# Projections in five pieces of 512 columns, gate and up with sixteen little products in a row, and a planner that knows the turns of VectorE and GpSimd

## The chip, the core and the metric

One core of a Trainium2 chip runs the whole program in one launch. The metric is the device time in microseconds (us) of one execution. TensorE multiplies matrices into PSUM, ScalarE (ACT) and VectorE (DVE) work elementwise on SBUF and PSUM, GpSimd (POOL) works elementwise on SBUF, and SyncE (SP) issues most of the DMAs.

## What is computed

Two encoder layers over 256 tokens of width 1024, in float32. Cut to what matters:

```python
def mixer_sublayer(x, ...):
    proj = rms_norm(x, n1) @ w_in_l                      # 1024 -> 2560 columns
    qa, ka, va, qd, kd, vd, qc, kc, vc = split(proj)     # 4+4+4, 6+6+6, 6+2+2 heads of 64
    out_a = neighbourhood_attention(norm(qa), norm(ka), va, rpb)
    out_d = dilated_window_attention(rope(norm(qd)), rope(norm(kd)), vd)
    out_c = gqa_block_attention(rope(norm(qc)), rope(norm(kc)), vc)
    mix = concat(rms_norm(out_a), rms_norm(out_d), rms_norm(out_c))
    return x + mix @ w_out_l

def channel_sublayer(x, ...):
    g, u = split(rms_norm(x, n2) @ w_gu)                 # 1024 -> 2 x 2816
    g = depthwise_conv_centred(g, cw, cb)                # three taps along the tokens
    return x + (gelu(g) * u) @ w_dn
```

## The kernel before

**Precision.** Every float32 operand is split into a large part `hi` (a cast to fp32r) and a rest `lo`. A product a·b is three matmuls, hi·hi, hi·lo and lo·hi (`mm3`). ScalarE makes `hi` of each weight chunk (`wp_hi`), VectorE the rest (`wp_lo`). The token rows lie in two tiles t of 128.

**Projections.** `PROJ` cuts the 2560 columns of `w_in` into seven pieces: dq, dk, dv and cq of 384 columns, ckv of 256, aqk of 512, av of 256. A piece takes 2 (t) × 8 (k, chunks of 128 rows) × 3 matmuls into two PSUM banks of the pool `psa`, with the split activations `act_hT` as weights in the array and the split `w_in` streaming through it. A load unit is one DMA into a `raw` buffer (four exist): four chunks k of a piece of 384 or 512 columns, eight of a piece of 256.

**Attention.** The `weave` runs the projections, and after them the output projections (`act_mixT` with `w_out`), as filler between the steps of 16 heads: norm and rotation of queries and keys (`normed`, `rotated`, tile `act_z`), transposes (`transposed`), score products with half the array (64 rows), softmax, transposes of the probabilities, and weighing of the values (`const_v`). For the dilated heads `rotated` takes tables that GpSimd makes from the norm gains (`tables_d`).

**Gate and up.** `half_up` makes two PSUM banks j = 0, 1 of the pool `psw`. For each bank there are eight large products (wp_hi with both parts of `act_hT`, 512 columns) and eight little ones (wp_lo with the large part, 256 columns). The order is large 0, little 0, large 1, little 1. There are 22 calls in each layer; the first of a layer has an order of its own. `down` stands between them, with 24 products of 512 columns for two tiles j.

**Order.** Nothing runs as it is written: the class `Plan` records all operations, and `order` lists them by estimated start times from `cost`, with hand-written shifts of rank in `PLACES`. Every engine then works through its own list strictly in order. `LANDS` holds the times at which the planner takes the first loads to be landed. All recorded operations carry the line L472, the call in `emit`, so the profile is read by tile names.

```python
            for j in range(2):
                for k in range(KD):
                    large(j, k)
                for k in range(KD):
                    little(j, k)
```

Of the kernel before, what the change touches and what calls it, by code (L numbers as in the profile page):

```python
# [18 lines left out]
P = 128  # L19
# [32 lines left out]
LANDS = (4100, 3300, 5300, 3450, 5800, 6450, 7250, 8200, 8900, 9800, 10700, 10750, 10800)  # L52
# [4 lines left out]
SUM_ACT, SCALE_ACT = ("dq", "dk", "cq"), ("dk",)  # L57
# [9 lines left out]
PROJ_NAMES = ["dq", "dk", "dv", "cq", "ckv", "aqk", "av"]  # L67
PROJ = [
    (_CD, _WD), (_CD + _WD, _WD), (_CD + 2 * _WD, _WD), (_CC, H_GQ * HD),
    (_CC + H_GQ * HD, 2 * GKV_W), (0, 2 * H_NA * HD), (2 * H_NA * HD, H_NA * HD),  # L70
]

OUTP = [(2, 3), (5, 3), (0, 2)]
# [132 lines left out]
class Op:  # L206
    __slots__ = ("engine", "method", "args", "kw", "ns", "lat", "kind", "size", "tiles", "first", "before", "after", "left", "at", "rank", "burst")
# [17 lines left out]
def handover(a, b):  # L225
# [13 lines left out]
class Plan:  # L239
# [30 lines left out]
    def add(self, engine, method, args, kw):  # L270
# [16 lines left out]
        o.ns, o.lat, o.size, o.kind = cost(engine.name, method, args, kw, ins)  # L287
        func = args[2] if method == "activation" else None
# [34 lines left out]
    def order(self):  # L323
# [9 lines left out]
        wires = {}  # L333
        ready = {e: [] for e in ("PE", *free)}
# [68 lines left out]
        while len(done) < len(ops):  # L403
# [71 lines left out]
def cost(engine, method, args, kw, ins):  # L475
# [11 lines left out]
    if engine == "PE":  # L487
        if method == "transpose":
            return n / 2.25 + 2.5, 0, 0, "turn"
        n = args[2].width()  # L490
        ns = {512: 231.6, 384: 174.5, 256: 118.0}.get(n, n / 2.25 + 2.5)
# [14 lines left out]
    elif method == "tensor_copy":  # L506
        ns = 0.92 * n + 100
    elif kw.get("op") == ALU.pow:
        ns = 560 + 150 * n
    elif method == "tensor_scalar":  # L510
        ns = 350 + 3.8 * n
    else:
        ns = 830 if out.width() == S else 350 + 3.1 * n
    return ns, ns - 95, 0, None


@with_exitstack
def encoder_kernel(
# [70 lines left out]
    with nc.later(1000):  # L589
# [8 lines left out]
        [const.tile([P, NT, 2 * n + 1, HD], F32R, tag=f"v{n}{i}", name=f"v{n}{i}") for i in range(2)]  # L598
        for n in (H_DIL, H_GKV)
    )  # L600
    for z in vown + vkv:
        nc.gpsimd.memset(z[:, :, 0::2].bitcast(F32), 0.0)

    def rows(w, k0, n, c0, width):
        return w[k0 * P : (k0 + n) * P, c0 : c0 + width].rearrange("(k p) c -> p k c", p=P)

    def units_of(l):

        for c0, width in PROJ:
            per = 4 if width * 8 > UNIT else 8  # L610
            for k0 in range(0, KD, per):
                yield rows(w_in[l], k0, per, c0, width)
        for gi, c0 in OUT_ORDER:
            yield rows(w_out[l], *OUTP[gi], c0, 512)
        for kind, s in FFN:
            if kind == "D":
                yield rows(w_down[l], 2 * s, 2, 0, D)
            else:
                yield rows(w_gate_up[l], 0, KD, (D_FF if kind == "U" else 0) + s * 2 * P, 2 * P)
# [8 lines left out]
    def keep(i):  # L628
        v = views[i]
        a, b = v.shape[1], v.shape[2]  # L630
        n = a * b
        raw = wp.tile([P, UNIT], F32, tag="raw", name=f"raw{i}", bufs=RAWS)
        nc.sync.dma_start(raw[:, :n].rearrange("p (a b) -> p a b", b=b), v)
# [10 lines left out]
    def load(i):  # L644
        v = views[i]
        a, b = v.shape[1], v.shape[2]
# [10 lines left out]
        rv = raw[:, : a * b].rearrange("p (a b) -> p a b", b=b)  # L657
        if i == 0:
            for by, what, c in START:
                by = nc.scalar if by == "act" else nc.sync  # L660
                if what == "w":
                    by.dma_start(rv[:, c], v[:, c])
# [7 lines left out]
        else:  # L670
            for c in range(0, a, 2 if i == 1 else a):
                e = c + 2 if i == 1 else a
                nc.sync.dma_start(rv[:, c:e], v[:, c:e])
        raws.append(raw)

    def places_of(i):
# [4 lines left out]
        return (16, 16) if views[i].shape[2] == 2 * P else (0, 0)  # L681

    def split(i):
        v = views[i]
        a, b = v.shape[1], v.shape[2]
# [170 lines left out]
    def tables_d(l, which):  # L856
        cd = act.tile([P, NT, HD], F32, tag=f"cd{which}", name=f"cd{which}{l}", bufs=1)
        sd = small.tile([P, NT, 16], F32, tag=f"sd{which}", name=f"sd{which}{l}", bufs=1)
        b = lambda v: v.unsqueeze(1).to_broadcast([P, NT, v.shape[1]])
        nc.gpsimd.tensor_tensor(cd, gains_of["rot"][:, :, 0:64], b(gains_of[which][:, l, 1]), op=ALU.mult)  # L860
        for i in range(2):
            o, n = (8 * i, 8 * (1 - i)), 8
            nc.gpsimd.tensor_tensor(
                sd[:, :, o[0] : o[0] + n],
                gains_of["rot"][:, :, 64 + o[0] : 64 + o[0] + n],
                b(gains_of[which][:, l, 1, o[1] : o[1] + n]),
                op=ALU.mult,
            )
        return cd, sd
# [21 lines left out]
    def tables_of(l):  # L891
        for which in "qk":
            tables["d" + which, l] = tables_d(l, which)
# [4 lines left out]
    for l in range(DEPTH):  # L898
# [11 lines left out]
        def projections():  # L910
            for (c0, width), name in zip(PROJ, PROJ_NAMES):
# [649 lines left out]
```

## Time and profile before

| | us |
|---|---|
| median of 3 runs | 604.35 (604.31 to 604.79) |
| the profiled execution | 604.39 |
| its span, first to last instruction | 602.6 |
| PE busy in the span | 596.9 (99%), 3496 matmuls |
| DVE busy | 484.9 (80%) |
| ACT busy | 428.5 (71%) |
| POOL busy | 81.0 (13%) |

The profiled execution is the span and 1.8 us around it. Busy times of PE are unions of overlapping matmuls, each of which is drawn with its way through the array; how fast the array takes matmuls is read from the distance of their starts.

### The profile page before, as it was taken

How to read it: one execution, taken by the hardware profiler on the slowest of the kernel's cores; microseconds unless marked ns; L12 is line 12 of the kernel's file. 1: busy time of each engine (PE TensorE's matmuls, PEld its weight loads, DVE VectorE, ACT ScalarE, POOL GpSimd, SP SyncE). 2: the span in 40 equal slices, each digit the busy share in tenths (PEclk: the TensorE clock that was granted, in tenths of full speed). 3: DMA queues.
4: the chain of work that ended last, by engine and by line, in shares of the span. 5: the costliest groups of instructions: out<-in, count | busy, mean ns of one | idle time of the engine just before them, and what ended most of it. 6: DMA issues, size and time to landing. Idle time of an engine off the chain costs nothing.

```text
span 602.6 us, 9916 instructions
## 1 busy us (share of the span) xinstructions
PE 596.9 (99%) x3496; PEld 524.7 (87%) x3496; DVE 484.9 (80%) x995; ACT 428.5 (71%) x1065; POOL 81.0 (13%) x130
## 2 busy tenths in 40 slices
PE   8999999999999999999999999999999999999997
PEld 7999898888888888888899989888888888888886
DVE  4899988997788988888777898777977777777775
ACT  6889999686566767666688899676766556666661
POOL 2733030102400000000023213421000000000000
PEclk9999999999999999999999999999999999999999
DMA  8893313557588898999444726844465556555501
GB/s 281 294 329 114 106 36 108 196 188 238 174 243 292 274 358 310 327 308 298 155 143 159 258 71 245 281 177 140 140 210 202 171 188 210 173 179 208 194 16 70
DMA packets 85218, 121.44 MB, mean 202 GB/s; under 512 B 9881, under 2 KB 69881, under 8 KB 85169
## 3 DMA queue, kind: packets, MB, share of 16 engines
q1 hardware_dynamic: 82896, 112.17, 55.8%
q0 software_dynamic: 1728, 8.39, 4.1%
q8 instruction: 27, 0.44, 0.3%
q10 hardware_dynamic: 544, 0.26, 0.1%
q14 instruction: 23, 0.18, 0.1%
HBM read 110.93 MB, written 9.88 MB: 200 GB/s over the span
## 4 chain that ended last, share of the span: by engine, by line
PE 97%; ACT 1%; DVE 1%; POOL 0%; issue 0%; DVEq 0%; POOLq 0%
PE psw_w L472 53%; PE psa_a L472 44%; ACT act_s2k L472 0%; POOL small_rstd L472 0%; ACT act_z L472 0%; DVE act_z L472 0%; ACT act_hT L472 0%; DVE wp_lo L472 0%; DVE act_sw L472 0%; POOL small_ms L472 0%; DVE const_x L472 0%; DVE act_qo L472 0%; ACT wp_hi L472 0%; POOL const_warm L472 0%; DVEq L472 0%
## 5 line engine op out<-in xcount | busy, mean ns | idle before, releaser
L472 DVE TENSOR_TENSOR wp_lo<-wp_raw,wp_hi 128x512 fp32r<-128x512 f32 (+2 forms) x332 | 231.8, 733 | 57.1 <-ACT wp_hi L472 41.1
L472 ACT CAST wp_hi<-wp_raw 128x512 fp32r<-128x512 f32 (+2 forms) x332 | 203.0, 663 | 21.7 <-PE psw_w L472 10.1
L472 PE MATMUL psw_w<-act_hT,wp_hi 128*128 128x512 f32 x704 | 180.3, 393 | 0.0
L472 PEld LDWEIGHTS psw_w<-act_hT,wp_hi 128*128 128x128 f32 x704 | 127.3, 188 | 24.5 <-DVE act_hT L472 0.6
L472 PE MATMUL psa_a<-wp_hi,act_hT 128*128 128x384 f32 (+2 forms) x448 | 112.6, 331 | 0.7 <-ACT wp_hi L472 0.7
L472 PEld LDWEIGHTS psw_w<-act_hT,wp_lo 128*128 128x128 f32 x704 | 97.2, 188 | 7.1
L472 PE MATMUL psw_w<-act_hT,wp_lo 128*128 128x256 f32 x704 | 101.3, 280 | 0.0
L472 PEld LDWEIGHTS psa_a<-wp_hi,act_hT 128*128 128x128 f32 x448 | 78.2, 188 | 3.4 <-ACT wp_hi L472 0.9
L472 PE MATMUL psa_a<-wp_lo,act_hT 128*128 128x384 f32 (+2 forms) x224 | 74.2, 333 | 0.1
L472 ACT COPY act_s2k<-psw_w 128x256 f32<-128x256 f32 x88 | 32.3, 372 | 58.5 <-PE psw_w L472 58.1
L472 PE MATMUL psa_a<-wp_lo,act_ch 128*128 128x512 f32 (+1 forms) x176 | 68.2, 387 | 0.0
L472 PE MATMUL psa_a<-wp_hi,act_ch 128*128 128x512 f32 x176 | 68.1, 388 | 0.0
L472 PE MATMUL psa_a<-wp_hi,act_cl 128*128 128x512 f32 (+1 forms) x176 | 67.6, 388 | 0.0
L472 DVE TENSOR_TENSOR act_s2k<-psw_w,act_s2k 128x256 f32<-128x256 f32 x88 | 36.7, 422 | 12.2 <-ACT act_s2k L472 11.8
L472 PEld LDWEIGHTS psa_a<-wp_lo,act_hT 128*128 128x128 f32 x224 | 42.1, 188 | 2.3 <-DVE wp_lo L472 1.0
L472 PEld LDWEIGHTS psa_a<-wp_hi,act_cl 128*128 128x128 f32 x176 | 33.1, 188 | 6.8
L472 PEld LDWEIGHTS psa_a<-wp_hi,act_ch 128*128 128x128 f32 x176 | 33.0, 188 | 6.2
L472 PEld LDWEIGHTS psa_a<-wp_lo,act_ch 128*128 128x128 f32 x176 | 33.1, 188 | 6.0
L472 DVE SCALAR_TENSOR_TENSOR act_s2k<-act_s2k,act_cw,act_s2k 128x255 f32<-128x255 f32 x88 | 36.8, 478 | 1.4 <-ACT act_s2k L472 1.3
L472 ACT ACTIVATE act_s2k<-act_s2k 128x512 f32<-128x512 f32 x22 | 13.9, 632 | 30.2 <-DVE act_s2k L472 30.2
L472 ACT ACTIVATE act_s2k<-act_s2k,act_cw 128x256 f32<-128x256 f32 x44 | 24.1, 595 | 15.4 <-DVE act_s2k L472 15.4
L472 POOL TENSOR_TENSOR small_rstd<-small_ms,const_mh 128x6 f32<-128x6 f32 (+2 forms) x26 | 30.8, 1186 | 14.2 <-DVE small_ms L472 12.6
(132 smaller groups left out, 791.7 us busy)
## 6 DMA issues: line engine op xcount, KB each, us to landing
wp_raw<-in_w_gate_up_dram SPq DMA_DIRECT2D x44, 1024.0 KB, 5.0
wp_raw<-in_w_down_dram SPq DMA_DIRECT2D x22, 1024.0 KB, 7.3
wp_raw<-in_w_in_dram SPq DMA_DIRECT2D x14, 768.0 KB, 5.9
wp_raw<-in_w_in_dram SPq DMA_DIRECT2D x8, 1024.0 KB, 7.0
wp_raw<-in_w_out_dram SPq DMA_DIRECT2D x8, 768.0 KB, 7.8
dram_khi<-act_mixT_hi SPq DMA_DIRECT2D x4, 768.0 KB, 3.6
dram_klo<-act_mixT_lo SPq DMA_DIRECT2D x4, 768.0 KB, 8.4
wp_lo<-dram_klo POOLq DMA_DIRECT2D x4, 768.0 KB, 5.0
```

The costliest lines, as they stand in the source:

```text
L472: getattr(o.engine.real, o.method)(*map(real, o.args), **{k: real(v) for k, v in o.kw.items()})
```

## The change

It does four things.

1. `PROJ` has five pieces of 512 columns: d0 (four query and four key heads of the dilated group), d1 (two and two, with four value heads), cq (two value heads and the six queries of group c), akv (values of a, keys and values of c) and aqk. A piece can gather several column ranges, and a load unit is then two or three DMAs (`Unit.load`). The prep, the transposes and the value tiles follow: `prep_d` and `turn_d` handle query and key heads together, `const_v` has three slots for two heads, and the values of group a are made at head 3 instead of head 10.
2. In `half_up` bank 1 begins with its little products, so that sixteen little ones stand in a row.
3. The planner holds back a VectorE operation with two SBUF inputs while GpSimd works, and GpSimd while VectorE does (`port`, `held`). Costs in `cost`, `LANDS` and all of `PLACES` are new.
4. Half of the heads' scaling in `normed` is done on ScalarE for d0 and d1, in place of all of dk's.

```diff
-LANDS = (4100, 3300, 5300, 3450, 5800, 6450, 7250, 8200, 8900, 9800, 10700, 10750, 10800)
+LANDS = (4100, 3300, 5300, 3450, 6000, 6900, 7700, 8800, 9700, 10600, 11500, 11550, 11600)
...
-PROJ_NAMES = ["dq", "dk", "dv", "cq", "ckv", "aqk", "av"]
+PROJ_NAMES = ["d0", "d1", "cq", "akv", "aqk"]
 PROJ = [
-    (_CD, _WD), (_CD + _WD, _WD), (_CD + 2 * _WD, _WD), (_CC, H_GQ * HD),
-    (_CC + H_GQ * HD, 2 * GKV_W), (0, 2 * H_NA * HD), (2 * H_NA * HD, H_NA * HD),
+    [(_CD, 4 * HD, _WD, 2)],
+    [(_CD + 4 * HD, 2 * HD, _WD, 2), (_CD + 2 * _WD, 4 * HD, 0, 1)],
+    [(_CD + 2 * _WD + 4 * HD, BANK, 0, 1)],
+    [(2 * H_NA * HD, H_NA * HD, _CC + H_GQ * HD - 2 * H_NA * HD, 2)],
+    [(0, BANK, 0, 1)],
 ]
...
 PLACES = {
-    375: -35, 488: 15, 528: -53, 550: 173, 587: -78, 594: 125, 616: -286, 646: -9, 709: -79, 750: -226, 752: -396,
...
+    69: 675, 174: 69, 175: 485, 176: 81, 201: 382, 299: 271, 372: 236, 390: 27, 400: 25, 409: 64, 508: 25, 568: 374,
...
-                free[e], end = at + o.ns, at + o.lat
+                wait = 0.0
+                if o.port == "both":
+                    wait = max(0.0, held["POOL"] - at)
+                    held["DVE"] = at + wait + o.ns
+                elif o.port:
+                    wait = max(0.0, held["DVE"] - at - 100)
+                    held["POOL"] = at + wait + (o.ns if o.port == "long" else 160)
+                free[e], end = at + wait + o.ns, at + wait + o.lat
...
+        def load(self, by, raw, ks):
...
+            if many > 1:
+                pieces = [(c0 + i * step, width, 0, 1) for c0, width, step, n in pieces for i in range(n)]
+            for c0, width, step, n in pieces:
...
+                by.dma_start(dst, bass.AP(tensor=self.w.tensor, offset=offset, ap=ap))
...
         hooks = {
-            (0, 0): lambda: (wv.until("cq"), prep_c("q", gq)),
+            (0, 0): lambda: (rest_d(), prep_c("q", gq)),
             (2, 0): lambda: turn_c("q"),
-            (3, 0): lambda: (wv.until("ckv"), prep_c("k", gk)),
+            (3, 0): lambda: (wv.until("akv"), prep_c("k", gk), values_a()),
...
-            for j in range(2):
-                for k in range(KD):
-                    large(j, k)
-                for k in range(KD):
-                    little(j, k)
+            for j, kinds in enumerate(((large, little), (little, large))):
+                for part_ in kinds:
+                    for k in range(KD):
+                        part_(j, k, part_ is kinds[0] and k == 0, part_ is kinds[1] and k == KD - 1)
```

In the whole program the lists of instructions hold 3304 matmuls in place of 3496 (192 fewer, all of them projections), 161 DMAs on SyncE in place of 149, and on ScalarE and VectorE 48 casts and 48 subtractions of 512 columns in place of 64 and 64 of 384.

On TensorE, in the middle of layer 1, one gate unit and one up unit stood like this (`psw_w` is the bank of one j):

```order
L472 MATMUL psw_w_166<-act_hT_146,wp_hi_141 128x512 x8
L472 MATMUL psw_w_166<-act_hT_146,wp_lo_149 128x256 x8
L472 MATMUL psw_w_83<-act_hT_146,wp_hi_240 128x512 x8
L472 MATMUL psw_w_83<-act_hT_146,wp_lo_248 128x256 x8
L472 MATMUL psw_w_124<-act_hT_146,wp_hi_240 128x512 x8
L472 MATMUL psw_w_124<-act_hT_146,wp_lo_248 128x256 x8
```

and stand now:

```order
L496 MATMUL psw_w_117<-act_hT_148,wp_hi_142 128x512 x8
L496 MATMUL psw_w_117<-act_hT_148,wp_lo_255 128x256 x8
L496 MATMUL psw_w_124<-act_hT_148,wp_lo_255 128x256 x8
L496 MATMUL psw_w_124<-act_hT_148,wp_hi_142 128x512 x8
L496 MATMUL psw_w_170<-act_hT_148,wp_hi_244 128x512 x8
L496 MATMUL psw_w_170<-act_hT_148,wp_lo_150 128x256 x8
L496 MATMUL psw_w_83<-act_hT_148,wp_lo_150 128x256 x8
L496 MATMUL psw_w_83<-act_hT_148,wp_hi_244 128x512 x8
```

The little blocks of the two banks meet, and so do the large blocks of neighbouring calls.

On TensorE, at the end of the first load unit (`const_warm` is a filler product that computes nothing, `act_s2k` by `const_ident` a small transpose), before:

```order
L472 MATMUL psa_a_175<-wp_lo_149,act_hT_146 128x384
L472 MATMUL psa_a_175<-wp_hi_141,act_hT_146 128x384
L472 MATMUL psw_w_166<-const_ident_89,act_s2k_130 128x32
L472 LDWEIGHTS const_warm_77
L472 MATMUL psw_w_83<-const_warm_77 128x256
L472 MATMUL psa_a_157<-wp_hi_240,act_hT_146 128x384
```

The same place now (`wp_hi_142` holds the first load unit, `wp_hi_244` the second):

```order
L496 MATMUL psa_a_160<-wp_hi_142,act_hT_148 128x512 x2
L496 MATMUL psa_a_160<-wp_lo_150,act_hT_148 128x512
L496 MATMUL psa_a_160<-wp_hi_142,act_hT_148 128x512
L496 MATMUL psw_w_124<-const_ident_89,act_s2k_130 128x32
L496 MATMUL psa_a_156<-wp_hi_244,act_hT_148 128x512
L496 MATMUL psa_a_160<-wp_hi_244,act_hT_148 128x512
L496 MATMUL psa_a_156<-wp_lo_255,act_hT_148 128x512
```

No filler stands there any more; all 28 fillers stand ahead of the first projection product, where 27 stood.

On GpSimd, at the start of layer 0 (`act_nab` is a copy for the bias of group a, `act_cd` and `small_sd` the tables for the rotation of group d, `small_rstd` the norms of the heads), before:

```order
L472 TENSOR_SCALAR small_ms_300<-small_ss_284,small_he_263 128x6
L472 TENSOR_TENSOR act_cdq_305<-const_rot_170,const_gq_178 128x128
L472 TENSOR_TENSOR small_sdq_316<-const_rot_170,const_gq_178 128x2x8 x2
L472 TENSOR_TENSOR small_rstd_328<-small_ms_300,const_mh_85 128x6
L472 TENSOR_SCALAR small_ms_344<-small_ss_311,small_he_263 128x6
L472 TENSOR_TENSOR small_rstd_351<-small_ms_344,const_mh_85 128x6
L472 TENSOR_TENSOR act_cdk_369<-const_rot_170,const_gk_184 128x128
L472 TENSOR_TENSOR small_sdk_381<-const_rot_170,const_gk_184 128x2x8 x2
L472 COPY act_nab_394<-small_few_192 28x1984
```

and now:

```order
L496 COPY act_nab_303<-small_few_198 28x1984
L496 TENSOR_SCALAR small_ms_329<-small_ss_292,small_he_260 128x8
L496 TENSOR_TENSOR small_rstd_338<-small_ms_329,const_mh_85 128x8
L496 TENSOR_SCALAR small_ms_356<-small_ss_318,small_he_260 128x8
L496 TENSOR_TENSOR act_cd_363<-const_rot_206,const_gk_217 128x2x64
L496 TENSOR_TENSOR small_sd_372<-const_rot_206,const_gk_217 128x2x8 x2
L496 TENSOR_TENSOR small_rstd_379<-small_ms_356,const_mh_85 128x8
L496 TENSOR_TENSOR act_cd_363<-const_rot_206,const_gq_238 128x2x64
L496 TENSOR_TENSOR small_sd_372<-const_rot_206,const_gq_238 128x2x8 x2
```

The long copy moved ahead of the norms, and the table of the query gains behind both of them.

## Rows read from the trace of the kernel before

**Rows 1.** The page, parts 1 and 2: engines over the span, granted clock.

```profile
PE 596.9 (99%) x3496; PEld 524.7 (87%) x3496; DVE 484.9 (80%) x995; ACT 428.5 (71%) x1065; POOL 81.0 (13%) x130
...
PEclk9999999999999999999999999999999999999999
```

**Rows 2.** Timeline, PE, seven-piece projections: start, length, instructions of 384 columns.

```profile
22.15 0.51 PE L472 MATMUL psa_a<-wp_hi,act_hT 128*128 128x384 f32 x2
...
24.23 0.51 PE L472 MATMUL psa_a<-wp_hi,act_hT 128*128 128x384 f32 x2
```

**Rows 3.** Timeline, PE, the piece ckv in layer 1 (256 columns).

```profile
342.91 0.40 PE L472 MATMUL psa_a<-wp_hi,act_hT 128*128 128x256 f32 x2
...
347.11 0.39 PE L472 MATMUL psa_a<-wp_hi,act_hT 128*128 128x256 f32 x2
```

**Rows 4.** Timeline, PE, the piece aqk in layer 1 (512 columns).

```profile
351.08 0.40 PE L472 MATMUL psa_a<-wp_lo,act_hT 128*128 128x512 f32 x1
...
353.14 0.29 PE L472 MATMUL psw_w<-act_ch,const_v 128*128 128x256 f32 x1
```

**Rows 5.** Timeline, PE, one gate, the up behind it, then down.

```profile
438.13 1.98 PE L472 MATMUL psw_w<-act_hT,wp_hi 128*128 128x512 f32 x8
439.95 1.10 PE L472 MATMUL psw_w<-act_hT,wp_lo 128*128 128x256 f32 x8
440.89 2.02 PE L472 MATMUL psw_w<-act_hT,wp_hi 128*128 128x512 f32 x8
442.75 1.11 PE L472 MATMUL psw_w<-act_hT,wp_lo 128*128 128x256 f32 x8
443.69 1.98 PE L472 MATMUL psw_w<-act_hT,wp_hi 128*128 128x512 f32 x8
...
449.26 0.40 PE L472 MATMUL psa_a<-wp_hi,act_ch 128*128 128x512 f32 x1
...
454.71 1.52 PE L472 MATMUL psw_w<-act_hT,wp_hi 128*128 128x512 f32 x6
```

**Rows 6.** Timeline, PE, the start: first load unit and the hole behind it.

```profile
7.30 0.44 PE L472 MATMUL psa_a<-wp_hi,act_hT 128*128 128x384 f32 x1
...
13.21 0.28 PE L472 MATMUL psw_w<-const_warm 128*128 128x256 bf16 x1
14.16 0.62 PE L472 MATMUL psa_a<-wp_hi,act_hT 128*128 128x384 f32 x2 [0.67 <-ACT wp_hi L472]
14.76 0.44 PE L472 MATMUL psa_a<-wp_lo,act_hT 128*128 128x384 f32 x1
15.04 0.51 PE L472 MATMUL psa_a<-wp_hi,act_hT 128*128 128x384 f32 x2
```

**Rows 7.** Timeline, ACT, the start.

```profile
12.98 0.64 ACT L472 ACTIVATE act_s2k<-const_x 128x512 f32<-128x512 f32 x1
...
13.59 3.40 ACT L472 CAST wp_hi<-wp_raw 128x384 fp32r<-128x384 f32 x8
```

**Rows 8.** Busy time of each engine in two stretches.

```profile
core 0: us, PE busy (x) PEld busy (x) DVE busy (x) ACT busy (x) POOL busy (x), PEclk, DMA share, GB/s
18.00:28.00 10.00, 10.00 (x59) 10.00 (x59) 7.88 (x18) 7.74 (x46) 8.69 (x13) 1.00 1.01 355
95.30:111.00 15.70, 15.70 (x99) 13.85 (x98) 12.99 (x37) 13.54 (x39) 1.46 (x2) 1.00 0.22 71
```

**Rows 9.** Timelines of POOL, DVE and PE: copy, rotation, first head transposes.

```profile
24.11 2.16 POOL L472 COPY act_nab<-small_few 28x1984 f32<-28x1984 f32 x1
...
22.53 0.32 DVE L472 TENSOR_TENSOR act_sw<-act_z,small_sdq 128x48 f32<-128x48 f32 x2
...
24.49 1.96 DVE L472 TENSOR_TENSOR act_sw<-act_z,small_sdq 128x48 f32<-128x48 f32 x2
...
28.56 0.81 PE L472 MATMUL psw_w<-const_ident,act_z 128*128 128x128 f32 x6
```

**Rows 10.** Timelines of PE and DVE, the end of the program.

```profile
598.27 0.39 PE L472 MATMUL psa_a<-wp_hi,act_cl 128*128 128x512 f32 x1
...
596.88 0.48 DVE L472 SCALAR_TENSOR_TENSOR const_x<-psw_w,small_rx,const_x 128x256 f32<-128x256 f32 x1
598.70 0.75 DVE L472 SCALAR_TENSOR_TENSOR const_x<-psa_a,small_rx,const_x 128x512 f32<-128x512 f32 x1 [1.34 <-PE psa_a L472]
```

More of the change, by code (lines that the diff above doesn't have):

```diff
@@ L206 @@
 class Op:
-    __slots__ = ("engine", "method", "args", "kw", "ns", "lat", "kind", "size", "tiles", "first", "before", "after", "left", "at", "rank", "burst")
+    __slots__ = ("engine", "method", "args", "kw", "ns", "lat", "kind", "size", "tiles", "first", "before", "after", "left", "at", "rank", "burst", "port")
 class PlanEngine:
@@ L506, in cost, with port @@
     elif method == "tensor_copy":
-        ns = 0.92 * n + 100
+        ns = 0.98 * n + 100
     elif kw.get("op") == ALU.pow:
-        ns = 560 + 150 * n
+        ns = 380 + 157 * n
     elif method == "tensor_scalar":
-        ns = 350 + 3.8 * n
+        ns = 270 + 1.7 * n
     else:
-        ns = 830 if out.width() == S else 350 + 3.1 * n
+        ns = 180 + 2.19 * n
     return ns, ns - 95, 0, None
+def port(engine, method, kw, ins):
+    inside = [v for v in ins if not v.tile.pool.psum]
+    if engine == "DVE" and method in ("tensor_tensor", "scalar_tensor_tensor"):
+        wide = [v for v in inside if v.width() > 1]
+        return "both" if len(wide) == 2 and len(inside) == len(ins) else None
+    if engine == "POOL" and method in ("tensor_tensor", "tensor_scalar", "tensor_copy"):
+        return "short" if kw.get("op") == ALU.pow else "long"
+    return None
 @with_exitstack
@@ L607, in units_of @@
     def units_of(l):
[L609 to L612, printed above, removed]
+        for pieces in PROJ:
+            for k0 in range(0, KD, 4):
+                yield Unit(w_in[l], k0, 4, pieces)
         for gi, c0 in OUT_ORDER:
-            yield rows(w_out[l], *OUTP[gi], c0, 512)
+            yield Unit(w_out[l], *OUTP[gi], [(c0, 512, 0, 1)])
         for kind, s in FFN:
@@ L661, in load @@
                 if what == "w":
[L662 removed]
+                    v.load(by, raw, slice(c, c + 1))
                 elif what == "x":
@@ L891, in tables_of @@
     def tables_of(l):
-        for which in "qk":
-            tables["d" + which, l] = tables_d(l, which)
+        tables["d", l] = tables_d(l)
         for which in "qk":
@@ L1050, in transposed, with by_pairs, values @@
             nc.vector.tensor_tensor(o, pv, h.bitcast(F32), op=ALU.subtract)
-        def by_pairs(what, group, n, zs, first=0):
-            c = "c" if group == "c" else "o"
+        def by_pairs(what, n, zs, first):
             both = [
-                act.tile([P, 3, S], F32R, tag=f"{what}{c}{i}", name=f"{what}{i}{group}{l}", bufs=1)[:, :n]
-                for i in range(2)
+                act.tile([P, 3, S], F32R, tag=f"{what}c{i}", name=f"{what}{i}c{l}", bufs=1)[:, :n] for i in range(2)
             ]
             for t in range(NT):
-                transposed(pairs(zs[t], first, n), both, t, f"{what}{group}{l}{t}")
+                transposed(pairs(zs[t], first, n), both, t, f"{what}c{l}{t}")
             return both
-        def values(places, src, t):
+        def values(places, src, t, runs):
             hi, lo = places
@@ L1242, in scores @@
                         scored[n] = sps
-                        g = two[0].group
+                        (q, qs), (k, ks) = (slots[two[0].group + w] for w in "qk")
                         for t in range(NT):
@@ L1256, in encoder_kernel @@
         for h in range(H_DIL):
-            heads.append(Head("d", h, h, [dil[:, t] for t in range(NT)], beside_zeros(vown, h, h % 2)))
+            heads.append(Head("d", h, h, [dil[:, t] for t in range(NT)], own(h)))
         for h in range(H_GQ):
@@ L1261, in encoder_kernel @@
         for h in range(H_NA):
[L1262 to L1266 removed]
+            heads.append(Head("a", h, h, na_bias(h), own(H_DIL + h)))
         groups = [(gi, h) for gi, n in enumerate((H_DIL, H_GQ, H_NA)) for h in range(n)]
```

239 lines of the change are left out of this document (139 added, 100 removed), and 20 rows, old and new, of the table PLACES.

## The prediction

> **What bounds the kernel now.** The page's engine table comes first: TensorE is busy 596.9 of 602.6 us, VectorE 80%, ScalarE 71%, and the clock row reads 9 in every slice, the full 2.4 GHz level from its first work on [rows 1]. So the next thing to read is the pace at which the array takes products, and it is read from the distance of starts, since drawn lengths overlap.
> - Twelve products of 384 columns take 24.23 − 22.15 = 2.08 us: 173.3 ns each [rows 2].
> - Thirty-six of 256 take 347.11 − 342.91 = 4.20 us: 116.7 ns [rows 3].
> - Nine of 512 (the first starts at 351.08; the row at 353.14 is the first instruction behind them) take 2.06 us: 228.9 ns [rows 4]. In down, 24 take 454.71 − 449.26 = 5.45 us: 227.1 ns [rows 5].
> - A gate or up unit lasts 443.69 − 438.13 = 5.56 us. Its blocks start at distances of 1.82 (large 0), 0.94 (little 0), 1.86 (large 1) and 0.94 us (little 1): large 1, right behind a little block, costs 0.04 us more than large 0, which also follows a little block, that of the unit before [rows 5].
>
> Then the windows: PE is never idle in either of the two busiest stretches, 10.00 of 10.00 and 15.70 of 15.70 us [rows 8]. TensorE waits in two places only: a hole at the start, from the filler at 13.21 to 14.16, where the profile names ScalarE's cast [rows 6], and nothing at the end but the evacuation and store behind the last product [rows 10]. Time can therefore go only from the number and pace of products, from that hole, and from the ends.
>
> **The change part by part**, against the profiled execution, 604.39 (the median shown is 604.35; 0.04 apart).
>
> *A. Five pieces.* For one tile t, one chunk k and one of the three products, the 2560 columns took 4 × 173.3 + 2 × 116.7 + 228.9 = 1155.5 ns and take 5 × 228.9 = 1144.5 ns, so 11.0 ns less. There are 2 × 8 × 3 × 2 layers = 96 such groups: **−1.06 us**. The columns are the same, so only what a product costs above its columns is saved, and 192 products fewer are only two in each group. Bounds: with the pace of down, 227.1, the five take 1135.5 and the term is −1.9; if the transitions between pieces eat the gain, 0. I take the projections' own pace, the nearest row.
> By the Trainium skill, "TensorE: Matmul & The Clock Gate", section "Back-to-back issue gap", a product at full clock takes N/2.4 and a fixed 2.5 ns; two fewer would save 5 ns × 96 = 0.5 us. The rows here lie 10.0, 13.3 and 15.6 ns above N/2.4 at 256, 384 and 512 columns, so the excess isn't fixed; the trace decides, and by the page the sum would be 0.6 us later.
>
> Casts and subtractions: 48 of 512 columns instead of 64 of 384, the same elements, on engines that PE doesn't wait for. Nothing, while that stays so [rows 1].
>
> *B. The start.* The hole lies between the first load unit and the second [rows 6]. The first unit's products (four chunks, three products, two t: 24) are now 512 wide: 24 × (228.9 − 173.3) = 1.33 us more work in front of the hole of 14.16 − 13.21 = 0.95 us. Against it: the second unit's casts, eight in 3.40 us and the first of them at 13.59, behind an activation of 0.64 us [rows 7], get a third more columns each, about 0.43 → 0.57 us; and a unit is 256 KB larger, 0.74 us at the 355 GB/s of the busiest window [rows 8]. I take **−0.75**, most of the hole; bounds −0.95 (all of it) and +0.3 (load and cast together, 0.74 + 0.14 late, with the 1.33 us of work used only in part because chunks arrive one by one).
>
> *C. Sixteen little products.* Of the four passages between blocks in a unit and its neighbour two are left. Large 1 costs 0.04 us over large 0 [rows 5]. Whether that price belongs to the passage from little to large or to bank 1 itself, the rows of before can't tell: large 0 follows a little block too and doesn't pay. If it is the passage inside a unit, 42 regular units × 0.04 = −1.7 us; if it is the bank, 0. That large 0 shows no price at its passage speaks for the bank; I take a value nearer to 0, **−0.4**, bounds 0 and −1.7.
>
> *D. Last heads' cover.* The order puts 29 output products in place of 39 between the last scores and the last weighing in layer 0, and 26 in place of 32 in layer 1, each 512 wide as before: about 10 × 228.9 ns = 2.3 us and 6 × 228.9 = 1.4 us less cover for softmax. In layer 0's stretch ScalarE works 13.54 of 15.70 us while PE waits for nothing [rows 8], so 2.16 us of slack face 2.3 us less cover. I take **+0.3**; bounds 0 and +3.7 (both covers lost in full).
>
> *E. The end.* PE now finishes in products 256 wide, and the last evacuation is one of 256 columns: 0.48 in place of 0.75 us [rows 10], −0.27. The last store is half as large. No row here splits a store into its fixed part and its bytes; 0 to 0.4 us, and I take −0.23. Together **−0.5**, bounds −0.2 and −0.7.
>
> *F. The planner's turns, `PLACES`, costs, ScalarE's half of the scaling.* They move work on engines that are not the bound. What hides them is TensorE's uninterrupted queue; in the window where VectorE's 0.32 us product grew to 1.96 beside GpSimd's copy of 2.16 [rows 9], PE was busy all through [rows 8]. So the better turns are worth 0 by themselves. If a turn comes late at the first transposes they cost, and that is the second rival.
>
> Sum: −1.06 − 0.75 − 0.4 + 0.3 − 0.5 = −2.4; 604.4 − 2.4 = **602.0 us**.
>
> **The rivals.**
>
> *Flat, 603.4.* The pace of 512 columns isn't 228.9 but 230.0 in the mix of units (A: 1155.5 − 1150.0 = 5.5 ns × 96 = −0.5), C is nothing, the hole is only moved (B 0), the end gives −0.5: 604.4 − 1.0. For it: 512 shows the largest excess over N/2.4 of all widths here. Against: the hole has a plain cause and gets more work in front. The fixed price of the Trainium skill's page, above, would make A alone come out so.
>
> *All of it, 599.1.* A at −1.9, B at −0.95, C at −1.7 and the end at −0.7 give −5.25, with D at nothing. For it: down shows 227.1, and large 1 shows its 0.04 in each unit. Against: both prices must turn out to be those that the change removes.
>
> *A new wait in layer 0, 606.0, the other side.* Place: the first transposes of group d, on TensorE. They need the rotated queries, VectorE's rotation needs the tables that GpSimd makes, and GpSimd's list now has the copy of 2.16 us [rows 9] ahead of the norms and the table of the query gains behind both norms. Those gains are loaded behind the first units, in a stretch whose DMA engines are already full (share 1.01, [rows 8]). TensorE comes to the transposes after some 75 projection products from 14.75 on, 14.75 + 75 × 0.2289 = 31.9, against 28.56 before [rows 9]; it has 3.4 us more in front, and GpSimd's own work grows by 2.16 ahead of the table. If the table is late beyond that, everything behind waits in order, since TensorE takes its list as it stands. It gives 602.0 + 4 = 606.0 with a wait of 4 us; it turns the gain at 2.4 us of wait and is a measurable loss from 3.6 us. Against it: 3.4 us of room is more than the 2.16 us that move ahead.
>
> *It doesn't do what it says.* The count can't fail: 192 products are gone from TensorE's list. The turns may do nothing in the trace, which leaves the sum as it is (F is zero).
>
> **How the numbers follow.** Main case 602.0: 0.55. Flat 603.4: 0.20. All 599.1: 0.13. New wait 606.0 (or the same at D): 0.12. About 0.2% (1.2 us) is what a measurement of this kernel can tell from no change. The main case, with its terms at independent places inside their bounds, spreads from 600.8 to 603.6 or so, and a tenth of it lies within 1.2 us of 604.35; flat lies half on either side of 603.15, a little more within; "all" is faster throughout; of the new wait 0.10 is slower. Faster: 0.49 + 0.09 + 0.13 + 0.01 = 0.72; same 0.06 + 0.11 + 0.01 = 0.18; slower 0.10. The range leaves out most of the new wait (0.10) and about two thirds of "all" (0.08): 599.6 to 604.0.
>
> **What would show each step.** A: nine 512-wide products in the first pieces at 2.06 us, or 2.04 with the pace of down; 2.08 and over would leave flat. B: no idle between fillers and the second unit, and a last filler ahead of the first product. C: distances between the four blocks of a unit; if large 1, now last, still costs 0.04 over large 0, the price is the bank's, and if one of the two falls to the other it was the passage's. D: idle of PE ahead of the last weighings of each layer, with ScalarE or VectorE named. E: the row of the last evacuation, 0.48, and the time from it to the end of the span. The rival: an idle of TensorE ahead of the first transposes at about 32 us, released by VectorE's rotation or GpSimd's table. The prediction is wrong if PE shows holes of over 1 us anywhere between 16 us and the end, or if the widest products turn out to have another pace than in the rows of before.

## The result and the profile after

The changed kernel takes 606.34 us (median of 19 runs, 605.04 to 608.28) against 604.31 (19 runs, 603.26 to 605.28): ratio 1.0035, 95% interval 1.0027 to 1.0043. It is 2.0 us slower, where 2.4 us faster were forecast. Its runs also lie further apart, 3.2 us against 2.0; the slowest, 608.28, has a mean granted clock of 0.996 where the others have 0.999 or 1.000. Its profiled execution, 605.31, is one of its fastest; it stands 0.92 above that of before.

The page of the changed kernel: engines, granted clock, and the chain of work that ended last.

```profile
PE 595.9 (99%) x3304; PEld 505.3 (84%) x3304; DVE 484.2 (80%) x991; ACT 425.2 (70%) x1049; POOL 86.7 (14%) x130
...
PEclk9999999999999999999999999999999999999999
...
PE 77%; DVE 6%; POOL 5%; DMA 5%; issue 3%; ACT 3%; SPq 1%; DVEq 0%; POOLq 0%; ACTq 0%
```

TensorE has 192 products fewer and is busy 1.0 us less than in [rows 1], at the same clock. But the chain is no longer TensorE alone: in before PE had 97% of it, and now almost a quarter leads through other engines and DMAs. TensorE's waits in the same trace (releaser, total, times, longest):

```profile
PE psw_w L496 <- POOL const_warm L496: 1.0, 1, 1.0
PE psa_a L496 <- DMA wp_lo<-dram_klo: 0.8, 1, 0.8
PE psa_a L496 <- DMA wp_hi<-dram_khi: 0.6, 1, 0.6
PE psw_w L496 <- DVE act_hT L496: 0.4, 2, 0.2
PE psa_a L496 <- ACT act_hT L496: 0.3, 1, 0.3
PE psw_w L496 <- ACT act_s2k L496: 0.2, 1, 0.2
```

The same view of before had two lines: the first one here, and the hole of [rows 6]. The hole is gone, and five others have come.

Where the time went, from the distances of TensorE's starts in the two profiled executions (us):

| stretch | before | after | difference |
|---|---|---|---|
| first work to the first gate product of layer 0 | 118.80 | 117.83 | −0.97 |
| of it projections | 58.41 | 57.28 | −1.13 |
| of it output products | 22.95 | 24.00 | +1.05 |
| first to last gate or up product of layer 0 | 172.87 | 172.59 | −0.28 |
| from there to the first gate product of layer 1 | 122.20 | 124.39 | +2.19 |
| of it projections | 57.42 | 56.26 | −1.16 |
| of it output products | 23.21 | 25.07 | +1.86 |
| from there to the start of the last product | 183.43 | 183.71 | +0.28 |
| from there to the end of the span | 4.33 | 4.02 | −0.31 |

The projections give more than was forecast. Layer 1's attention takes back three times its gain, and in both layers the 96 output products, as many and as wide as before, take longer.

**The reads.** Both kernels split layer 1's output weights ahead of time, store them in DRAM (`dram_khi`, `dram_klo`) while layer 0's feed-forward runs, and read them back on GpSimd's queue. The prediction doesn't mention these reads: in the trace of before nobody waits for them. After, TensorE comes to its output products 5.8 us earlier (372.95, before at 378.77), and two of them wait. TensorE's timeline, and the two pieces of the chain that end in them (start, length):

```profile
372.95 0.40 PE L496 MATMUL psa_a<-wp_hi,act_mixT_hi 128*128 128x512 f32 x1
374.11 0.50 PE L496 MATMUL psa_a<-wp_lo,act_mixT_hi 128*128 128x512 f32 x1 [0.77 <-DMA wp_lo<-dram_klo]
...
394.31 0.50 PE L496 MATMUL psa_a<-wp_hi,act_mixT_hi 128*128 128x512 f32 x1 [0.60 <-DMA wp_hi<-dram_khi]
```

```profile
365.52 8.54 DMA wp_lo<-dram_klo
385.28 8.98 DMA wp_hi<-dram_khi
```

Both reads are 768 KB and take 8.5 and 9.0 us. What runs beside them is in the DMA view of 365.0 to 366.5 (queue, count, KB each, us from issue to landing), and for the second one in the windows (last two columns: DMA share, GB/s):

```profile
wp_raw<-in_w_down_dram SPq DMA_DIRECT2D x1, 1024.0 KB, 8.9
wp_hi<-dram_khi POOLq DMA_DIRECT2D x1, 768.0 KB, 5.7
wp_lo<-dram_klo POOLq DMA_DIRECT2D x1, 768.0 KB, 8.5
```

```profile
367.00:372.00 5.00, 5.00 (x43) 4.28 (x42) 2.71 (x6) 3.21 (x12) 0.00 (x0) 1.00 1.01 379
382.00:387.00 5.00, 5.00 (x41) 4.39 (x40) 4.54 (x10) 3.88 (x12) 3.41 (x6) 1.00 1.07 357
387.00:392.00 5.00, 5.00 (x42) 3.96 (x40) 3.45 (x8) 2.88 (x9) 1.83 (x3) 1.00 1.09 391
```

The first down weights (1 MB, SyncE) are issued between the first two reads, and four reads of 512 KB that are needed only from 406.30 us on stand in the queue around the later one (three ahead of it, one behind). The DMA engines are full, by a share of 1.01 to 1.09.

### The profile page after: what moved, and what is told of

Its sections match the earlier page's. It is cut to its first block, busy times and chain, and to the rows that moved or that the text cites. A ratio compares the mean times of both kernels' runs of the same rounds, so it can differ in the third digit from the quotient of the medians.

```text
span 603.5 us, 9483 instructions
## 1 busy us (share of the span) xinstructions
PE 595.9 (99%) x3304; PEld 505.3 (84%) x3304; DVE 484.2 (80%) x991; ACT 425.2 (70%) x1049; POOL 86.7 (14%) x130
## 4 chain that ended last, share of the span: by engine, by line
PE 77%; DVE 6%; POOL 5%; DMA 5%; issue 3%; ACT 3%; SPq 1%; DVEq 0%; POOLq 0%; ACTq 0%
PE psw_w L496 47%; PE psa_a L496 30%; POOL small_rstd L496 2%; ACT act_s2k L496 2%; DVE const_x L496 1%; DMA wp_hi<-dram_khi 1%; DMA wp_lo<-dram_klo 1%; SPq L496 1%; DVE wp_lo L496 1%; DVE act_z L496 1%; DMA const_x<-in_x_dram 1%; DMA small_few<-in_rpb_dram 1%; POOL small_ms L496 1%; DVE act_s2k L496 1%; ACT wp_hi L496 0%
## 5 line engine op out<-in xcount | busy, mean ns | idle before, releaser
L496 DVE TENSOR_TENSOR wp_lo<-wp_raw,wp_hi 128x512 fp32r<-128x512 f32 (+1 forms) x316 | 233.4, 767 | 43.6 <-ACT wp_hi L496 38.8
L496 ACT CAST wp_hi<-wp_raw 128x512 fp32r<-128x512 f32 (+1 forms) x316 | 201.7, 689 | 28.4 <-PE psw_w L496 21.2
L496 PE MATMUL psa_a<-wp_hi,act_hT 128*128 128x512 f32 x320 | 104.1, 398 | 0.3 <-ACT act_hT L496 0.3
L496 PE MATMUL psw_w<-act_hT,wp_lo 128*128 128x256 f32 x704 | 96.4, 279 | 0.0
L496 PEld LDWEIGHTS psa_a<-wp_hi,act_hT 128*128 128x128 f32 x320 | 59.1, 188 | 12.3 <-ACT act_hT L496 0.5
L496 PE MATMUL psa_a<-wp_hi,act_ch 128*128 128x512 f32 (+1 forms) x176 | 67.6, 388 | 0.0
L496 PE MATMUL psa_a<-wp_lo,act_hT 128*128 128x512 f32 x160 | 62.8, 395 | 0.0
L496 PEld LDWEIGHTS psa_a<-wp_lo,act_hT 128*128 128x128 f32 x160 | 30.1, 188 | 6.1 <-DVE wp_lo L496 0.2
L496 POOL TENSOR_TENSOR small_rstd<-small_ms,const_mh 128x2 f32<-128x2 f32 (+3 forms) x26 | 32.3, 1242 | 14.1 <-DVE small_ms L496 12.5
L496 ACT ACTIVATE act_s2k<-act_s2k,small_rs 128x256 f32<-128x256 f32 x64 | 29.2, 511 | 0.8 <-DVE small_rs L496 0.7
```

Of the source, the lines that this page charges most:

```text
L496: getattr(o.engine.real, o.method)(*map(real, o.args), **{k: real(v) for k, v in o.kw.items()})
```

## The experiments

The kernel before was measured again beside each experiment (medians 604.2 to 604.4); after's 606.34 is the one above. Except where it is said, each experiment keeps the planner's order and changes only what its diff shows.

**e1_short and e2_before_short: the eight reads cut short.**

```diff
+                if o.engine.name == "POOL" and o.method == "dma_start" and o.args[0].tile.pool.pool.name == "wp":
+                    args = [a[:, :64] for a in args]
```

> The changed kernel in the same order, but the eight reads of the stored output weights (768 KB each, GpSimd's queue, layer 1) fetch 64 of 1536 columns, so the products there work on old data. In the trace of the changed kernel TensorE waits 0.77 us for wp_lo<-dram_klo at 374.11 and 0.60 us for wp_hi<-dram_khi at 394.31. Theory: these reads are what made the kernel slower; without them about 1.7 us go in the profile and more in the median, whose runs scatter upwards: 606.3 falls to 604.3 or less, and no DMA is named in TensorE's waits. Rival: the loss is spread over the attention steps (waits of 0.1 to 0.4 us for ScalarE and VectorE); then the time stays at 605.5 or above.

> The kernel before with the same eight reads cut to 64 columns, so the products there work on old data. Its trace shows no wait of TensorE for them. Theory: the time stays at 604.3, within 0.3 us. Rival: the reads cost something through the DMA engines in any order; then it falls by 0.5 us or more.

e1 took 604.68 us (1.7 less than after), e2 603.89 (0.3 less than before, ratio 0.9993, interval 0.9984 to 1.0002). No DMA is left in e1's waits. So the reads cost 1.7 us after, and before nothing that stands clear of the interval. e1 missed its 604.3 a little: 0.4 us of loss and the whole forecast gain lie elsewhere.

**e3_reads and e6_reads2: the reads put in order.** Only GpSimd's list is changed, and one load goes there from SyncE; what is moved stays the same. The DMAs of that list around 381 us, after against e6 (in e3 `wp_hi_142` alone goes up, and `wp_raw_95` stands last too):

```diff
 DMA wp_lo_255<-dram_klo_2360
+DMA wp_hi_142<-dram_khi_2340
+DMA wp_hi_244<-dram_khi_2490
+DMA wp_lo_150<-dram_klo_2505
 DMA act_kc_908<-dram_klo_2641
 DMA act_kc_903<-dram_khi_2627
 DMA act_qc_679<-dram_khi_2757
-DMA wp_hi_142<-dram_khi_2340
 DMA act_qc_687<-dram_klo_2776
-DMA wp_hi_244<-dram_khi_2490
-DMA wp_lo_150<-dram_klo_2505
+DMA wp_raw_95<-in_w_down_dram
```

> The changed kernel with two moves in GpSimd's list: the read of wp_hi for the third output unit goes ahead of the four reads of 512 KB, and the load of the first down weights (1024 KB, which ran beside the first two reads) goes from SyncE to GpSimd's queue behind all reads. Theory: both waits shrink, 0.77 and 0.60 us in the profile; the time falls by 1.2 to 2 us, to 604.3 to 605.1. Rival (loss elsewhere): 605.8 to 606.5.

> As e3_reads, but the four reads of 512 KB and the load of the down weights come behind all eight reads of 768 KB in GpSimd's queue. In e3_reads the wait had moved to the last of the eight (1.0 us for wp_lo<-dram_klo at 400). Theory: no wait for these reads is left and the time is that of e1_short, 604.7. Rival: bytes, not order, set the landing (share 1.04 to 1.09 of the DMA engines from 382 to 397 us); then 605.2 to 606.

e3 took 605.69, between its theory's range and its rival's: the two waits were gone, but the 512 KB reads now delayed the fourth unit's (1.0 us for `wp_lo<-dram_klo`). e6 took 604.44 (ratio to before 0.9999, interval 0.9991 to 1.0008), 1.9 us less than after, as its theory has it. The first two reads landed in 4.8 and 5.9 us in place of 5.7 and 8.5:

```profile
wp_hi<-dram_khi POOLq DMA_DIRECT2D x1, 768.0 KB, 4.8
wp_lo<-dram_klo POOLq DMA_DIRECT2D x1, 768.0 KB, 5.9
```

TensorE's waits in e6, apart from the filler's:

```profile
PE psa_a L510 <- ACT act_hT L510: 1.7, 2, 1.5
PE psw_w L510 <- DVE act_hT L510: 0.4, 2, 0.2
PE psw_w L510 <- ACT act_s2k L510: 0.2, 1, 0.2
PE psw_w L510 <- DVE small_nm L510: 0.2, 1, 0.2
```

The loss against before is thus a matter of the order of transfers (and, for the down weights, of their queue), not of their bytes. The line with 1.5 us is new here, and belongs to the start.

**The start: what the traces tell.** Programs with the same front end differ in when the first chunk of `w_in` lands and ScalarE casts it. Each line below is one profiled execution (us):

| front end | first cast | first product of the second load unit |
|---|---|---|
| of before (e8) | 5.26 | 14.15 |
| of before (before) | 5.33 | 14.16 |
| of before (e2) | 5.87 | 14.20 |
| of before (e4) | 6.40 | 14.27 |
| of before, e12 | 6.69 | 14.55 |
| of after (after) | 5.24 | 14.13 |
| of after (e9) | 5.59 | 14.86 |
| of after (e3) | 6.52 | 15.37 |
| of after (e14) | 6.58 | 15.46 |
| of after (e1) | 6.62 | 15.49 |
| of after (e6) | 6.87 | 15.75 |
| of after, e13 | 6.60 | 15.49 |

In the front end of before, a cast 1.4 us later moves the second unit by 0.4; in that of after, 1.6 us later by 1.6. The pace of the fillers is not the reason: in after and in e6 alike they start 0.21 us apart up to 3.7 us and 0.11 apart from 4.3 on, and the second units lie 1.6 us apart. The reason can be read in TensorE's and ScalarE's rows. e12, with a late cast, still has the hole of [rows 6]:

```profile
6.69 0.51 ACT L476 CAST wp_hi<-wp_raw 128x384 fp32r<-128x384 f32 x1 [3.66 <-DMA wp_raw<-in_w_in_dram]
...
13.59 0.28 PE L476 MATMUL psw_w<-const_warm 128*128 128x256 bf16 x1
14.55 0.62 PE L476 MATMUL psa_a<-wp_hi,act_hT 128*128 128x384 f32 x2 [0.68 <-ACT wp_hi L476]
```

e6, with a late cast, has none; its products go through without a stop into the second unit:

```profile
6.87 0.62 ACT L510 CAST wp_hi<-wp_raw 128x512 fp32r<-128x512 f32 x1 [3.85 <-DMA wp_raw<-in_w_in_dram]
...
7.92 0.73 PE L510 MATMUL psa_a<-wp_hi,act_hT 128*128 128x512 f32 x2 [1.48 <-ACT act_hT L510]
...
15.25 0.40 PE L510 MATMUL psa_a<-wp_hi,act_hT 128*128 128x512 f32 x1
15.58 0.24 PE L510 MATMUL psw_w<-const_ident,act_s2k 32*128 32x32 f32 x1
15.75 0.74 PE L510 MATMUL psa_a<-wp_hi,act_hT 128*128 128x512 f32 x2
```

The hole was slack. The wider products filled it, so what used to end in it, a landing that varies by 1.6 us, now moves everything behind it. The whole times go along with that. With after's front end the profiled execution lies 1.03 us below its program's median with the cast at 5.24, 0.37 below with 5.59, and 0.02 to 0.56 above with the five casts from 6.52 on; with before's it lies 0.06 to 0.25 above, whenever the cast came. That is a trend over single executions and no more. The spread of after's runs is not shown to come from the start: e1 and e6, with the same front end, lie within 1.4 and 1.5 us.

**e12_before_late and e13_after_late: the first two chunks exchanged.**

```diff
+            first = [i for i in done if self.ops[i].engine.name == "SP" and self.ops[i].method == "dma_start"][:4]
+            done.remove(first[2])
+            done.insert(done.index(first[3]) + 1, first[2])
```

> The kernel before, with the loads of the first two chunks of w_in in exchanged order on SyncE, so that the one that ScalarE casts first is issued 0.5 us later and behind 192 KB. In four traces with this front end the first cast began at 5.26 to 6.40 and the second load unit's first product always at 14.16 to 14.27. Theory: the hole of 0.95 us ahead of the second unit is slack and takes this up; with a cast at about 7 the second unit starts at 14.2 to 14.7 and the time is 604.3 to 604.8. Rival: the landing counts in both kernels; then 605 to 605.8.

> The changed kernel with the same exchange (behind 256 KB). In its six traces the second unit starts 8.8 to 9.0 us behind the first cast, whenever that is. Theory: no slack is left, so a cast that is later by 0.8 to 1.5 us makes the whole later by as much: 607 to 608, second unit at 16 or later. Rival (the landing counts in both, or in neither): the same change of time as in e12_before_late.

e12 took 604.39 (ratio 1.0000, interval 0.9991 to 1.0009), as the theory has it. e13 took 606.53 and missed its 607 to 608, but its cast came at 6.60, no later than in the other runs of this front end, so it tested nothing. The two do not settle the matter; the twelve traces of the table do, for the second unit's start. How much of after's median that is stays open: in the six traces with after's own front end four casts lie 1.3 to 1.6 us behind the earliest, and one 0.35.

**e5_start and e7_both: the first chunk issued first.** (e7 is e5 and e6 together.)

```diff
+DMA wp_raw<-in_w_in_dram 128x2x256
 DMA act_s2k<-in_norm_g_dram 16x128
 DMA const_ident<-in_c_ident_dram 128x128
-DMA wp_raw<-in_w_in_dram 128x2x256
```

> The changed kernel with one move on SyncE: the load of the first chunk of w_in (256 KB) is issued first, ahead of the norm gains and of the identity, at about 0.73 us in place of 1.63. In three traces with the same front end ScalarE's first cast of this chunk began at 5.24, 6.62 and 6.52 us and the second load unit's first product at 14.13, 15.49 and 15.37; in three traces with the front end of before the cast began at 5.33, 5.87 and 6.40 and the second unit at 14.16, 14.20 and 14.27. Theory: in the changed kernel the landing of this chunk goes straight into the time, in the kernel before the hole ahead of the second unit takes it up; issued 0.9 us earlier, the cast begins at 5.7 or before, and the median falls by 0.5 to 1.0 us, to 605.3 to 605.8. Rival: what is late is the transfer itself (all first loads share the DMA engines), so the order of issue changes nothing: 606.0 to 606.6.

> The moves of e5_start and e6_reads2 together. Theory: they lie at different places and add, 603.8 to 604.3, the time of the kernel before or a little less. Rival (one of them does nothing): 604.7 or more.

e5 took 608.0, above both its ranges, and e7 604.99, in its rival's. The cast came at 4.37 and 4.20, but the identity, now behind 256 KB, came late, and the first transposes stood still:

```profile
PE psw_w L501 <- DMA const_ident<-in_c_ident_dram: 1.6, 1, 1.6
PE psa_a L501 <- DMA wp_lo<-dram_klo: 1.5, 1, 1.5
```

The theory that issuing earlier is enough falls: moving this load up moved the identity down. (The second line shows the reads again, at 1.5 us in this run.)

**e4_before_row and e8_before_row: the row of sixteen alone, in the kernel before.**

```diff
-for j in range(2): large(j, 0..7), little(j, 0..7)
+large(0, 0..7), little(0, 0..7), little(1, 0..7), large(1, 0..7)
```

> The kernel before in its own order, with only the row of sixteen little products: bank 1 begins with its little ones. In the trace of the changed kernel a gate or up unit lasts 5.563 to 5.574 us, against 5.557 to 5.567 before, and bank 1's large block is still the slower one. Theory (the price is the bank's): the time stays at 604.3, within 0.3 us. Rival (the price is the passage's): 602.6.

> The kernel before in its own order, only the row of sixteen little products: bank 1 begins with its little ones, and ScalarE's casts of the next unit stay behind the large products that read the same buffer. Theory (the price of the slower large block belongs to bank 1): 604.2, within 0.4 us. Rival (it belongs to the passage from little to large): 602.6.

e4, in which ScalarE's casts of a later unit stayed ahead of the large products that had moved behind them, took 634.80 and tests nothing but that (24.2 us of waits for `wp_hi`). e8 took 611.85. Its gate units last 5.563 to 5.574 us, as those of after. Of the 7.5 us over before, 4.7 are a wait at one place. Behind it the granted clock stood at half, 0.50, from 194.2 to 197.6 us, and products of 512 columns start 0.42 us apart in place of 0.23, which costs another 1.7 us (half of the stretch):

```profile
193.78 0.51 PE L515 MATMUL psw_w<-act_hT,wp_lo 128*128 128x256 f32 x2 [4.71 <-DVE wp_lo L515]
...
196.40 0.63 PE L515 MATMUL psa_a<-wp_lo,act_ch 128*128 128x512 f32 x1
196.82 0.63 PE L515 MATMUL psa_a<-wp_hi,act_ch 128*128 128x512 f32 x1
...
PEclk9999999999998999999999999999999999999999
```

The last line, from the page, has its only 8 in that slice. So the row itself saves nothing in a unit, and in an order not made for it it costs. Both theories missed.

**e10_no_turns and e11_column: parts of the change undone, and planned anew.**

```diff
 def port(engine, method, kw, ins):
+    return None
```

> The changed kernel without part 3's rule: the planner no longer holds VectorE and GpSimd back for each other, with everything else, PLACES too, as it is. The order then differs in some 170 rows of TensorE's 1901. By the prediction (the rule is worth nothing by itself) 605.3 to 607.3. Rival (the rule makes room for the moved norms and tables): 608 or more.

> The changed kernel with the order of the kernel before in half_up (large 0, little 0, large 1, little 1), planned anew. Theory (the row of sixteen is worth nothing, since a unit takes 5.57 us either way): 605.8 to 606.8. Rival (the row is what costs, by holding a weight buffer longer: in e8_before_row it cost 7.6 us where the order around it stayed as it was): 605 or less.

e10 took 627.13 and e11 612.60. Neither theory's range held, nor e11's rival; e10 lies in its rival's range, 608 or more, though far above 608. e10's waits, the four largest:

```profile
PE psw_w L496 <- ACT act_ch L496: 3.5, 2, 2.7
PE psw_w L496 <- DVE act_hT L496: 3.0, 2, 1.7
PE psw_w L496 <- ACT act_z L496: 2.4, 1, 2.4
PE psw_w L496 <- ACT act_s2k L496: 2.2, 3, 0.8
```

The shifts in `PLACES` are counted in numbers of recorded operations and fit one set of costs. With another rule or another order in `half_up`, the same shifts make another order, and it is worse by 6 to 21 us. A part of that is the clock: the granted clock fell to 0.50 twice in e10, behind waits of 2.7 and 2.4 us, and once in e11. What the rule is worth with shifts of its own can't be read from this, and stays open. That it is worth nothing, as the prediction had it, is not shown either.

**e9_moves and e14_best: the small waits.** e9 makes nine moves in the lists of e6 (eight on VectorE and ScalarE, and a load that has to follow), e14 the two at the end of layer 1 with that load:

```diff
 TENSOR_SCALAR small_ms
-TENSOR_TENSOR wp_lo<-wp_raw,wp_hi 128x512 x2
 SCALAR_TENSOR_TENSOR const_x<-psa_a,small_rstd,const_x 128x512
+TENSOR_TENSOR wp_lo<-wp_raw,wp_hi 128x512
 SCALAR_TENSOR_TENSOR const_x<-psa_a,small_rstd,const_x 128x512
+TENSOR_TENSOR wp_lo<-wp_raw,wp_hi 128x512
```

> e6_reads2 with eight more moves inside the lists of VectorE and ScalarE, for the waits that its trace still shows on TensorE and that the kernel before does not have: at 48.85 (0.37 us; the third head's maximum goes ahead of a scaling that waits for GpSimd, the reciprocal ahead of four rotation products), at 54.54 (0.35; the rest act_cl ahead of two maxima), at 119.78 (0.36; act_hT ahead of an update of x), at 412.00 and 415.07 (0.29 and 0.35; the first update of x ahead of two subtractions beside which GpSimd's 2-column power took 1.68 us instead of 0.69; act_hT ahead of an update of x, and ahead of a sum of squares). Theory: each of these waits is a matter of order on the feeding engine, and 1.0 to 1.7 us go: 602.7 to 603.4, below the kernel before. Rival: another operation is late next at the same places, and less than 0.5 us goes: 604.0 to 604.5.

> e6_reads2 with one of the moves of e9_moves alone: at the end of layer 1 the first and second update of x go ahead of two subtractions of wp_lo, so that GpSimd's 2-column power does not run beside them. Theory: the waits at 412.00 (0.29) and part of 415.07 (0.35) go and nothing else moves: 603.9 to 604.2, about the kernel before. Rival (as in e9_moves, the first gate unit waits instead): 604.4 or more.

e9 took 605.68, 1.2 us more than e6. The waits at 412 and 415 were gone, but others came, among them this one, where the distance of starts is 0.86 us over the usual (0.27 in e6):

```profile
53.78 0.63 PE L513 MATMUL psw_w<-const_ident,act_s2k 128*128 128x128 f32 x4 [0.70 <-DVE small_nm L513]
```

e14 took 604.62 (ratio to before 1.0001, interval 0.9992 to 1.0009), no better than e6: its wait at 412 is gone, and the one at 415 has grown from 0.35 to 0.76 us. e9 lies above its rival's range and e14 in its own rival's, and both traces show what the rivals said: another operation is late next. No version was found that beats the kernel before.

## Why the prediction was wrong

**What bounds the kernel, the step that failed.** "TensorE waits in two places only" was right of before and was carried over to after: "Time can therefore go only from" three things, and the sum has no term for a transfer that TensorE now meets too early. The runs show 1.7 us (e1) to 1.9 us (e6) there. The sentence said where time can go, not how near the next wait is. In before the first read pair had landed 3.8 us before it was needed. After, TensorE came 5.8 us earlier while the pair was issued only 2.8 us earlier, and its second read took 8.5 us in place of 6.7, with the 1 MB load now issued ahead of it instead of behind. (The clock's "full level from its first work on" holds for the products that the sum counts: in before the fillers start 0.21 us apart until 6.4 us, and 0.11 after.)

**A, right in direction, half in size.** Forecast −1.06, measured −1.13 and −1.16 by layer, −2.29. The pace of 512 was taken from an aqk piece that stands between attention steps [rows 4]; the first pieces, which now hold most of the products, run at the pace of down [rows 5]. In layer 1 after, 24 products:

```profile
310.01 0.39 PE L496 MATMUL psa_a<-wp_lo,act_hT 128*128 128x512 f32 x1
...
315.45 0.39 PE L496 MATMUL psa_a<-wp_lo,act_hT 128*128 128x512 f32 x1
```

5.44 / 24 = 226.7 ns, so 1155.5 − 5 × 226.7 = 22 ns for each of 96 groups, −2.1 us: a little beyond the term's lower bound of −1.9, which came from the pace of down, as the measured −2.29 is. Against the Trainium skill, "TensorE: Matmul & The Clock Gate", section "Back-to-back issue gap", the trace decided: 226.7 is 13.4 ns above 512 / 2.4, in place of the page's 2.5, and the two products fewer of a group saved more than 5 ns.

**B, mis-sized, and another size in each execution.** I booked the hole as time to be won. Its filling did happen: no filler stands between the units, and TensorE goes from the last product at 13.64 past a small transpose into the second unit at 14.13. In that execution the second unit starts where it did before, with 1.33 us more work done. But the bounds reached only from −0.95 to +0.3, and they priced loads by their mean rate, not by their scatter. With the landings of the other traces it starts at 14.86 to 15.75, so the term lies between about −1.4 (14.13, against 14.16 + 1.33) and +0.3; in five of the seven it is within 0.3 of nothing, where −0.75 was booked.

**C, the lower bound.** Forecast −0.4, measured 0: a unit took 5.57 us in the mean before and takes 5.57. TensorE after, in the middle of layer 1:

```profile
455.78 1.97 PE L496 MATMUL psw_w<-act_hT,wp_hi 128*128 128x512 f32 x8
457.59 2.05 PE L496 MATMUL psw_w<-act_hT,wp_lo 128*128 128x256 f32 x16
459.48 3.85 PE L496 MATMUL psw_w<-act_hT,wp_hi 128*128 128x512 f32 x16
463.17 1.10 PE L496 MATMUL psw_w<-act_hT,wp_lo 128*128 128x256 f32 x8
```

From large 0 to the next little 0: 463.17 − 455.78 = 7.39 us. By [rows 5] the same blocks took 5.56 + 1.82 = 7.38. The sixteen large ones take 3.69, not 2 × 1.81 = 3.62: the price went along with bank 1's block, as the words "or to bank 1 itself" allowed.

**D, mis-sized, and for the wrong place.** +0.3 was put on softmax at the end of attention. The output products took 22.95 and 23.21 us by layer before and 24.00 and 25.07 after. The reads explain about 1 us of that in the second (24.05 in e6). Of the other 1.9 us, three waits of about 0.3 us in e6's trace (by distances of starts) make 1.0; the rest is not explained. The bound of +3.7 held it; the wait that counted, for a DMA, isn't in the text. The end of layer 1 has a small one of another kind. GpSimd's power of two columns, 0.71 us before, took this long beside two of VectorE's subtractions:

```profile
410.15 1.68 POOL L496 TENSOR_TENSOR small_rstd<-small_ms,const_mh 128x2 f32<-128x2 f32 x1 [2.31 <-DVE small_ms L496]
```

**E, about right.** From the start of the last product to the end of the span: 4.33 us before, 4.02 after, 3.60 in e6; −0.3 to −0.7, forecast −0.5. The last evacuation is the 0.48 us that was expected:

```profile
599.83 0.48 DVE L496 SCALAR_TENSOR_TENSOR const_x<-psw_w,small_rx,const_x 128x256 f32<-128x256 f32 x1 [0.50 <-PE psw_w L496]
```

**F, not shown.** The chain through the first transposes, the rival with 0.12, did not come: they stand without a gap, and GpSimd's copy came early, at 18.71.

```profile
31.07 0.39 PE L496 MATMUL psa_a<-wp_hi,act_hT 128*128 128x512 f32 x1
31.30 0.60 PE L496 MATMUL psw_w<-const_ident,act_z 128*128 128x128 f32 x4
```

**The rivals and the chances.** The other side was looked for on VectorE and GpSimd's arithmetic. It came from GpSimd's DMA queue, which the prediction never opened: the DMA view of before lists the reads, with medians of 5.0 and 6.3 us. Slower had 0.10. That the rival of a new wait stood at 606.0, near the measured 606.34, is luck: its place, its engines and its 4 us are not what came. Nor did the prediction's own sign of being wrong show: the longest wait behind 16 us is 0.77 us, under the 1 us that it named.

**What stays open.** e6 has the reads in order and is still 2.4 us above the forecast. Of that, the start takes about 1.0 in executions with a late landing (+0.3 where −0.75 was booked), C 0.4; against it A gives 1.2 more. The rest is waits of 0.2 to 0.4 us in attention (by distances of starts over the usual ones), eight in e6 with 2.4 us in all where before had three with 0.6, and smaller ones in between. e9 shows that they aren't eight independent mistakes of order. Whether the pieces, the rule of turns or the shifts bring them isn't settled.

## What to carry to other kernels

When the bounding engine gets faster, list every transfer that it will meet earlier, with the time from landing to first use in the trace of before; that margin, not the engine's waits, says where the gain will stop. A hole in front of a step is worth its length only if nothing that varies from run to run ends in it: look at several traces of the same front end before booking it. And a hand-tuned order fits the one program it was tuned for; undoing a part by planning anew measures the misfit, so hold the order and move single instructions.

## What was not expected of the hardware

- Reads of 768 KB on GpSimd's queue landed after 4.8 us (e6, first pair in order) to 9.0 us (after, with the DMA engines full at a share of 1.07 to 1.09).
- The first load of `w_in`, issued at 1.63 or 1.64 us in all of these, was cast at 5.24 to 6.87 us in the six programs with the front end of after, which are alike up to there.
- The large block of bank 1 takes 1.86 to 1.87 us in place of 1.81 to 1.82 wherever it stands, right behind little products or in a row with the next unit's. In a few units it is the other block that is slow (before, at 198.77: 1.86 first, then 1.82). Its cause wasn't looked for.
- GpSimd's 2-column power took 0.71 us in e14, where VectorE stood still beside it, and 1.68 beside two subtractions of VectorE (after and e6).
- Behind a wait of 4.7 us (e8), and behind two of 2.7 and 2.4 us (e10), TensorE's granted clock stood at half for a stretch, and the time went up by more than the waits.
